# Where the first load stands in SyncE's opening instructions, in a ReLU-and-sum kernel on one core

## The chip, the cores and the metric

The kernel runs on one core of one Trainium2 chip. The metric is the time on the device in microseconds (us), the median of several executions. The span of a profile is another thing: it goes from the start of the first to the end of the last instruction that the profile ties to the kernel's source. In every profiled run of this case the time is 1.3 to 1.4 us longer than the span. "Faster" and "slower" mean a difference of over 2%, with 95% intervals.

## The reference

```python
def setup_inputs():
    batch, seq, dim = 32, 512, 1024
    return {"x": np.random.randn(batch, seq, dim).astype(np.float32)}

def reference(x):
    relu_x = np.maximum(x, 0)
    return np.sum(relu_x, axis=-1).astype(np.float32)
```

The input is 16,384 rows of 1,024 float32 values, 67.11 MB. The output is one number for each row.

## The kernel before

SyncE issues all loads and stores. The first seven loads bring 16 rows for each of 128 partitions (8.39 MB) into one of three buffers; the last 16 rows of each partition come as 8, 4, 2 and 1 rows, and the very last row in four pieces. ScalarE clamps the rows, VectorE sums them, or either does both for single rows. The first three loads wait for nothing; the fourth waits for the first buffer to come free (in the trace VectorE's first sum ends at 53.16 us and the fourth load is issued at 53.18).

The program opens with a block of its own, ahead of the kernel's body. In the trace of the kernel before it shows as four memsets on GpSimd, from 0.23 us on, and a barrier: each of the five engines has a drain, the last of them SyncE's, from 0.431 to 0.563 us, and after it come semaphore records: two of GpSimd at 0.590 and 0.668, then one of each other engine, SyncE's wait at 0.710 first, all ended by 0.772. In the program's text some register setup on SyncE stands there as well. The kernel edits that block after its body is written, and puts the first load into it, ahead of SyncE's part in the barrier:

```python
EARLY = 1
# ...
def issue_ahead_of_the_barrier(tc, n_loads):
    SP = mybir.EngineType.SP                      # SyncE
    blocks = tc.nc.main_func.blocks
    opening = blocks[0].instructions
    body = next(b for b in blocks if b.name == tc.start_bb_name).instructions
    loads = [i for i in body if i.engine == SP][:n_loads]
    for i in loads:
        assert isinstance(i, mybir.InstDMACopy)
        body.remove(i)
    at = next(
        n
        for n, i in enumerate(opening)
        if i.engine == SP and isinstance(i, mybir.InstDrain)
    )
    opening[at:at] = loads
```

This is safe because the load needs nothing of another engine: it reads the input and writes a buffer that nobody has touched. At that moment SyncE's part of the opening block is this list (the order is that of the program's text):

```text
MOVE             (a register)
BASE_LOAD        (the base address)
MOVE             (a register)
MOVE             (a register)
MOVE             (a register)
MOVE             (a register)
DRAIN
EVENT_SEMAPHORE  (the wait at the barrier)
branch to the kernel's body
```

## Time and profile before

| | before |
|---|---|
| time, median of 3 runs | 161.31 us (161.17 to 161.50) |
| span of the profiled run | 160.01 us |

The prediction reads the parts of the span and shows the lines for the shares and for the stages. A packet is one of the pieces in which a transfer moves; the profiled run has 2,592. The view of one source line adds what the opening of the program left in the profile. Its columns are line, engine, operation and count, then the shortest, median and longest record in ns, and the first and last start in us; a q behind an engine's name stands for its sequencer (the last column is for shapes, which these don't have):

```profile
L255 DVEq DRAIN  x1: 10/10/10, 0.1 to 0.1; - x1
L255 ACTq DRAIN  x1: 8/8/8, 0.1 to 0.1; - x1
...
L255 SPq DRAIN  x1: 132/132/132, 0.4 to 0.4; - x1
L255 SPq EVENT_SEMAPHORE  x1: 17/17/17, 0.7 to 0.7; - x1
```

The generated opening has records under one line, L255, and instructions as short as 8 ns are among them. SyncE has two of them, the drain and the wait, and no register move.

### The profile page before, as it was taken

To read this page: it belongs to the slowest core of one execution; us is meant where nothing else is said; L and a number is where in the kernel's file an instruction comes from. 1 tells how busy PE (TensorE), PEld (TensorE's weight loads), DVE (VectorE), ACT (ScalarE), POOL (GpSimd) and SP (SyncE) were. 2 spreads that over 40 slices of the span, in tenths; PEclk is the share of its full clock that TensorE was granted. 3 is DMA by queue.
4 is the path that set the end of the run, shared out by engine and by line. 5 is a ranking of instruction groups with operands and counts; after the bars stand their busy time and mean duration, and the time that the engine had idled before them with its cause. 6 is when DMAs were issued, how large, how long until landed. Compare 5 with 4: busy or idle time off the path is not lost.

```text
span 160.0 us, 135 instructions
## 1 busy us (share of the span) xinstructions
DVE 117.7 (74%) x43; ACT 104.2 (65%) x50; POOL 0.2 (0%) x4
## 2 busy tenths in 40 slices
DVE  0000000009999499994999999999999999999995
ACT  3000049990699808996099951999339992499993
POOL 0000000000000000000000000000000000000000
DMA  7996996996996997999979969969969969898993
GB/s 262 524 508 279 524 492 295 524 491 295 524 491 295 524 442 344 524 393 393 524 344 442 524 262 524 524 262 524 524 262 524 491 295 524 377 410 385 428 405 109
DMA packets 2592, 67.18 MB, mean 420 GB/s; under 512 B 672, under 2 KB 1184, under 8 KB 1312
## 3 DMA queue, kind: packets, MB, share of 16 engines
q1 hardware_dynamic: 2592, 67.18, 98.0%
HBM read 67.11 MB, written 0.07 MB: 420 GB/s over the span
## 4 chain that ended last, share of the span: by engine, by line
DMA 43%; DVE 33%; ACT 17%; another core or an unknown queue 3%; SPq 1%; issue 0%
DVE res L124 32%; DMA io<-in_x_dram 25%; DMA piece<-in_x_dram 18%; ACT io L116 17%; SPq L98 1%; DVE piece L141 1%; DVE piece L209 0%
## 5 line engine op out<-in xcount | busy, mean ns | idle before, releaser
L124 DVE TENSOR_REDUCE res<-io 128x8 f32<-128x8192 f32 (+2 forms) x9 | 101.1, 11291 | 40.2 <-ACT io L116 40.2
L116 ACT ACTIVATE io<-io 128x8192 f32<-128x8192 f32 (+2 forms) x9 | 81.7, 9111 | 47.2 <-DMA io<-in_x_dram 47.2
L131 ACT ACTIVATE io<-io 128x1024 f32<-128x1024 f32 x20 | 20.9, 1045 | 5.4 <-DMA io<-in_x_dram 5.3
L141 DVE TENSOR_SCALAR_CACHE_REDUCE io<-io 128x1024 f32<-128x1024 f32 x13 | 15.1, 1225 | 0.2
L131 ACT ACTIVATION_READ_ACCUMULATOR io<-io 128x1 f32 x20 | 3.7, 187 | 0.0
L116 ACT ACT_TABLE_LOAD x1 | 1.3, 1283 | 0.8 <-PEq L255 0.8
L141 DVE TENSOR_SCALAR_CACHE_REDUCE piece<-piece 128x244 f32<-128x244 f32 (+2 forms) x3 | 1.2, 415 | 0.5 <-DMA piece<-in_x_dram 0.5
L141 DVE DVE_READ_ACCUMULATOR io<-io 128x1 f32 x13 | 1.2, 93 | 0.0
L209 DVE TENSOR_SCALAR_CACHE_REDUCE piece<-piece 128x271 f32<-128x271 f32 x1 | 0.4, 435 | 0.0
L141 DVE DVE_READ_ACCUMULATOR piece<-piece 128x1 f32 x3 | 0.2, 83 | 0.0
L255 POOL MEMSET const-bfloat16-1.0<- 128x1 bf16 x1 | 0.1, 103 | 0.0
L255 POOL MEMSET const-uint8-127<- 128x1 uint8 x1 | 0.1, 103 | 0.0
L255 POOL MEMSET const-float32-1.0<- 128x1 f32 x1 | 0.1, 100 | 0.0
L255 POOL MEMSET const-float32-0.0<- 128x1 f32 x1 | 0.1, 99 | 0.2 <-issue 0.2
L209 DVE DVE_READ_ACCUMULATOR piece<-piece 128x1 f32 x1 | 0.1, 82 | 0.0
## 6 DMA issues: line engine op xcount, KB each, us to landing
io<-in_x_dram SPq DMA_DIRECT2D x1, 4096.0 KB, 21.6
io<-in_x_dram SPq DMA_DIRECT2D x1, 2048.0 KB, 26.1
io<-in_x_dram SPq DMA_DIRECT2D x1, 1024.0 KB, 28.1
io<-in_x_dram SPq DMA_DIRECT2D x1, 512.0 KB, 28.9
piece<-in_x_dram SPq DMA_DIRECT2D x1, 134.0 KB, 28.4
piece<-in_x_dram SPq DMA_DIRECT2D x1, 130.0 KB, 28.6
piece<-in_x_dram SPq DMA_DIRECT2D x1, 126.0 KB, 28.7
piece<-in_x_dram SPq DMA_DIRECT2D x1, 122.0 KB, 28.8
```

What stands on the lines that cost most here:

```text
L98: dma = nc.sync.dma_start(out=dst, in_=src)
L116: i = nc.scalar.activation(out=ap, in_=ap, func=RELU)
L124: nc.vector.tensor_reduce(out=res[:, m : m + n], in_=ap, axis=mybir.AxisListType.X, op=ADD).wait_op(sems.act, n_act, "sem-ge").then_inc(se ...
L131: i = nc.scalar.activation(out=ap, in_=ap, func=RELU, accum_out=res[:, m : m + 1])
L141: i = nc.vector.tensor_scalar(out=ap, in0=ap, scalar1=0.0, scalar2=None, op0=MAX, op1=ADD, accum_out=accum_out,)
L209: nc.vector.tensor_scalar(out=last[:, :], in0=last[:, :], scalar1=0.0, scalar2=None, op0=MAX, op1=ADD, accum_out=res[:, NT - 1 : NT],).wai ...
L255: nc = _bacc.Bacc("TRN2", target_bir_lowering=False, num_devices=1)
```

## The change

The intent: the load uses none of the six instructions at the head of SyncE's list, so it need not wait for them. It is to be SyncE's very first instruction.

```diff
-    at = next(
-        n
-        for n, i in enumerate(opening)
-        if i.engine == SP and isinstance(i, mybir.InstDrain)
-    )
+    at = next(n for n, i in enumerate(opening) if i.engine == SP)
     opening[at:at] = loads
```

## The prediction

> **What bounds the kernel now.** I read the page's busy shares first, then the table by stage, then the timeline of the start and of the end, and last the list of what each engine waited for. The page says that neither compute engine is full and that the transfers are:
>
> ```profile
> span 160.0 us, 135 instructions
> DVE 117.7 (74%) x43; ACT 104.2 (65%) x50; POOL 0.2 (0%) x4
> ...
> q1 hardware_dynamic: 2592, 67.18, 98.0%
> HBM read 67.11 MB, written 0.07 MB: 420 GB/s over the span
> ```
>
> VectorE works for 74% of the span, ScalarE for 65%, and the packets of the one DMA queue fill 98% of the time of the 16 engines. The table by stage shows where the missing 2% are (columns: stretch, its length, busy time of VectorE, ScalarE and GpSimd, granted clock, DMA share, GB/s):
>
> ```profile
> 0.00:1.00 1.00, 0.00 (x0) 0.21 (x1) 0.20 (x4) 1.00 0.00 0
> 1.00:4.00 3.00, 0.00 (x0) 1.07 (x1) 0.00 (x0) 1.00 1.03 350
> 4.00:156.00 152.00, 115.62 (x34) 101.42 (x46) 0.00 (x0) 1.00 1.00 432
> 156.00:160.00 4.00, 2.07 (x10) 1.53 (x4) 0.00 (x0) 1.00 0.40 110
> ```
>
> For the 152 us in the middle the DMA share is 1.00 at 432 GB/s: nothing but the transfer of the 67.11 MB input counts there. The first microsecond moves no byte, and the last four have a share of 0.40. I looked at the packets one by one: the first starts 1.02 us after the span's start, the last of the input ends at 157.70, and between these two there is not one moment without a packet in flight. So the kernel is a lead-in of 1.02, a stream of 156.68 (67.11 MB / 156.68 us = 428 GB/s), and a tail of 160.01 - 157.70 = 2.31 (the last sums, the last store, its landing). A change at the start of the program can reach the lead-in alone. The lead-in, in the timeline of SyncE's queue and of the others:
>
> ```profile
> 0.00 1.60 SPq L98 DMA_DIRECT2D io<-in_x_dram  x3
> 0.23 0.10 POOL L255 MEMSET const-float32-0.0<- 128x1 f32 x1 [0.23 <-issue]
> ```
>
> The span's zero is the issue of the first load itself: no SyncE instruction that the profile ties to the kernel's source stands before it. In the trace this first issue lasts 0.383 us; SyncE's drain for the opening barrier follows at 0.431, the barrier lets SyncE go at 0.71, and the second load is issued at 0.792. That is 20 us before the first load is in (ScalarE starts on it at 22.05), so the barrier is hidden behind the first transfer.
>
> [...] The trace[...] has 25 records on SyncE, 18 transfers, 6 semaphore instructions and 1 drain, and SyncE's compiled stream is 29 entries, these 25 and 4 markers of starts and branches. Not one register move is in either. [...] here the first packet starts at 1.02, which is 0.64 after its issue ends at 0.383[...]. [...] A semaphore instruction on SyncE lasts 17 ns in this trace.
>
> **The change part by part.** *Intended:* the first load goes from a place just ahead of SyncE's drain to the place of SyncE's first instruction. In the list of the opening block, as the kernel's code sees it when it makes the move, six SyncE instructions lie between the two: five register moves and one loading of the base address. [...]
>
> *What is left of it:* nothing in the load uses these six, and nothing else in the program does. The built program of the kernel before has none of them any more: the opening block ends up with 23 instructions, and SyncE's are the load, the drain, the wait of the barrier and the branch. They are removed after the kernel's code has made its move, in both versions. I compared the built programs engine by engine: the same instructions in the same order on all five engines, and only line numbers differ (the new file is four lines shorter). In the list of the new kernel the load stands ahead of GpSimd's four memsets and of the others' barrier instructions, where it stood behind them, but these are other engines' streams. I also compared what the compiler writes for each engine: the five instruction files are equal byte for byte.
>
> *Sum:* removed 0 instructions, added 0, moved 0 on any engine. Lead-in 1.02, stream 156.68 and tail 2.31 stay, so the span stays at 160.0 and the time at 161.31. I choose 161.3.
>
> **The rivals.** *First rival: the six instructions are executed, and the profile hides them.* For it: the profile shows only records tied to a source line, the span begins at the load, and the timed 161.37 of the profiled run is 1.36 us longer than its span of 160.01, so there is room ahead of the first record. Then the load would come 0.1 us (six at 17 ns)[...] earlier, the whole stream would move with it because it has no gap, and the time would fall to 161.0 to 161.2. Against it: the opening semaphore instructions and drains, which come from the same generated opening and carry the line L255, are in the trace, and moves of that origin would be too; and the compiled streams don't contain them.
>
> *Second rival: the load meets something else at the very start.* If it really were issued earlier, it would run before the other engines have arrived at the barrier, and SyncE's drain, which comes after the issue, would come earlier too[...]. The barrier is hidden behind 20 us of transfer, so this can neither gain nor cost. For a slowdown by over 2% (3.2 us) the stream itself would have to lose its 428 GB/s, and no byte, buffer, queue or wait of it is touched.
>
> *Third rival: the placing of code or data changes.* All buffers are allocated in the same order, and the streams are equal, so I give this almost nothing; a difference would be one between chips or runs.
>
> **Range and chances.** With nothing changed, the spread is that of repeated runs: 161.17 to 161.50, that is -0.09% and +0.12% about the median. A median of other runs, perhaps on another chip, should lie within about 0.35% of this one: 160.75 to 161.9. The low side also holds what the first rival could give. A change of 2% is 3.2 us, more than three times the whole lead-in of 1.02, so even a load that cost nothing at its start could not reach it: 0.98 for within 2%, and 0.01 for either side.
>
> **What would show it right or wrong.** The page of the changed kernel should have 135 instructions again, a span of 160.0 within 0.3, its zero at the first load's issue, the drain on SyncE at about 0.43 and the second load at about 0.79. First packet at 1.02 and no gap to about 157.7 would confirm the sum. If the first rival is true, the span stays (it starts at the load) but the time falls by 0.1 to 0.3 with it unchanged, so that the difference of 1.36 between the two gets smaller. The prediction would be wrong if the program that runs were built otherwise than the one I compared, with the moves kept, or if the stream's rate differed between the two.

The terms of its estimate for the six instructions came to 0.29 us, 0.2% of the time; one of them was measured in no trace. What is left with that estimate in it, the 161.0 of the first rival and the upper end of "0.1 to 0.3" here and in the first two expectations below (so also the 161.6 of the first), is the author's estimate; the lower end is six times the 17 ns that a semaphore instruction's record on SyncE lasts in the trace. The experiments measured 0.377 us. The forecast's own sum, lead-in 1.02, stream 156.68 and tail 2.31, comes to 160.01 us of span and 161.3 of time.

## The result, and the profile after

| | before | changed |
|---|---|---|
| time, median of 6 runs each | 161.30 us (161.13 to 161.50) | 161.26 us (161.18 to 161.58) |
| ratio, 95% interval | | 1.0001 (0.9988 to 1.0013) |
| span of the profiled run | 160.01 us | 159.83 us |
| first packet | 1.02 us | 1.02 us |
| second load issued | 0.792 us | 0.800 us |
| first buffer full, ScalarE starts | 22.05 us | 21.84 us |

A ratio is the mean time of one kernel's runs over that of the other's runs of the same rounds, so it is not quite the ratio of the medians. The time is the same.

The page of the changed kernel has the same number of instructions and the same busy times:

```profile
span 159.8 us, 135 instructions
...
DVE 117.7 (74%) x43; ACT 104.2 (65%) x50; POOL 0.2 (0%) x4
```

Its table by stage agrees as well (stretch, length, busy time of VectorE, ScalarE and GpSimd, granted clock, DMA share, GB/s):

```profile
0.00:1.00 1.00, 0.00 (x0) 0.21 (x1) 0.20 (x4) 1.00 0.00 0
1.00:4.00 3.00, 0.00 (x0) 1.08 (x1) 0.00 (x0) 1.00 1.04 350
4.00:156.00 152.00, 115.80 (x34) 101.59 (x46) 0.00 (x0) 1.00 1.00 432
156.00:160.00 4.00, 1.89 (x10) 1.35 (x4) 0.00 (x0) 1.00 0.40 109
```

And so does the timeline of its start:

```profile
0.00 1.61 SPq L98 DMA_DIRECT2D io<-in_x_dram  x3
0.23 0.10 POOL L251 MEMSET const-float32-0.0<- 128x1 f32 x1 [0.23 <-issue]
```

The zero is the first load's issue, as before, and GpSimd's first memset starts 0.23 us after it, as before. Had the load really come earlier against the rest of the program, this distance would have grown; in the experiments below the load does move against that memset, to 0.14 us behind its start with the six ahead of the load and to 2.12 with forty instructions there. The opening's line is now L251, since the file is four lines shorter; SyncE still has one drain and one wait there and no move:

```profile
L251 SPq DRAIN  x1: 141/141/141, 0.4 to 0.4; - x1
L251 SPq EVENT_SEMAPHORE  x1: 17/17/17, 0.7 to 0.7; - x1
```

The two profiled spans differ by 0.18 us. All of it is there when the first transfer is in, 21.84 against 22.05, long after both first packets at 1.02. Equal programs differ by that much from run to run: the times of the six runs of the changed kernel go from 161.18 to 161.58.

### The profile page after: what moved, and what is told of

Read it like the earlier page. It is cut to its first block, busy times and chain, and to the rows that moved or that the text cites. A ratio compares the mean times of both kernels' runs of the same rounds, so it can differ in the third digit from the quotient of the medians.

```text
span 159.8 us, 135 instructions
## 1 busy us (share of the span) xinstructions
DVE 117.7 (74%) x43; ACT 104.2 (65%) x50; POOL 0.2 (0%) x4
## 3 DMA queue, kind: packets, MB, share of 16 engines
HBM read 67.11 MB, written 0.07 MB: 420 GB/s over the span
## 4 chain that ended last, share of the span: by engine, by line
DMA 43%; DVE 33%; ACT 17%; another core or an unknown queue 3%; SPq 1%; issue 0%
DVE res L124 32%; DMA io<-in_x_dram 25%; DMA piece<-in_x_dram 18%; ACT io L116 17%; SPq L98 1%; DVE piece L141 1%; DVE piece L209 0%
## 5 line engine op out<-in xcount | busy, mean ns | idle before, releaser
L251 POOL MEMSET const-bfloat16-1.0<- 128x1 bf16 x1 | 0.1, 101 | 0.0
L251 POOL MEMSET const-uint8-127<- 128x1 uint8 x1 | 0.1, 101 | 0.0
L251 POOL MEMSET const-float32-0.0<- 128x1 f32 x1 | 0.1, 98 | 0.2 <-issue 0.2
L251 POOL MEMSET const-float32-1.0<- 128x1 f32 x1 | 0.1, 98 | 0.0
```

Of the source, the lines that this page charges most:

```text
L251: nc = _bacc.Bacc("TRN2", target_bir_lowering=False, num_devices=1)
```

## The experiments

The prediction says that the change moved nothing, as the six instructions are in neither program. Since the two compiled streams are equal byte for byte, the comparison is one of a program with itself, if what was compared is what ran. A result of "the same" fits that, but it alone would fit two other stories too: that the six are executed without records and cost too little to be seen, or that the place of the first load does not matter at all. The experiments put real instructions where the six had been thought to be.

### Keeping the six alive, with the load behind them

A use of the registers that the six instructions set is added to the kernel before, behind the third load, where SyncE has nothing to do for 51.6 us anyway. The use itself leaves no instruction, but the six now stay in the program. SyncE's compiled stream grows from 29 to 35 entries; the other engines' streams stay equal byte for byte to those of before.

```diff
+        if j == NBUF - 1:
+            keep_preamble_alive(nc)
...
+def keep_preamble_alive(nc):
+    sp = nc.sync
+    regs = [sp.zero_reg, *sp.tpb_base_reg]
+    for pair in sp.bc_regs:
+        regs += list(pair)
+    sp.keepalive_nop(ins=[sp.lower_val_access(r) for r in regs])
```

> The kernel before, with the six opening instructions of SyncE (five register moves, one loading of the base address) kept alive by a use behind the third load, so that they are executed ahead of the first load. Theory (they were not in either program; executed they cost something): six new records on SyncE ahead of the load, span and time longer by 0.1 to 0.3 us, 161.4 to 161.6, against 161.3. Rival (they are executed in the kernel before as well and only lack a record): the time stays at 161.3 and the first records stay as they were.

Measured: 161.50 us (161.44 to 161.71, 5 runs), before 161.25, ratio 1.0018 (1.0006 to 1.0031). The page counts six more instructions, and the view of the opening's line (L265 here) names them, as MOVE and BASE_LOAD:

```profile
span 160.4 us, 141 instructions
```

```profile
L265 SPq MOVE  x5: 29/29/40, 0.0 to 0.3; - x5
...
L265 SPq BASE_LOAD  x1: 12/12/12, 0.1 to 0.1; - x1
...
L265 SPq DRAIN  x1: 128/128/128, 0.8 to 0.8; - x1
```

The timeline puts the load behind them:

```profile
0.38 1.72 SPq L98 DMA_DIRECT2D io<-in_x_dram  x3
```

In the trace the six start at 0, 0.097, 0.144, 0.198, 0.257 and 0.307, and the load at 0.377; the first packet is at 1.386. So these instructions do leave records when they are executed, and they do cost time. The rival that the kernel before executes them unseen falls: it has neither the records nor the time.

### Keeping the six alive, with the load ahead of them

This is the changed kernel with the same addition, so the only difference to the experiment above is the diff under study.

> The changed kernel with the same six kept alive: the load is ahead of them. Theory: this is what the change was meant to do; the six run between the load and the drain, the barrier is later by their 0.1 to 0.3 us, hidden behind the first 20 us of transfer; time 161.3, so 0.1 to 0.3 less than with the load last. Rival (the place of the load does not matter even when the six are there): no difference between the two.

Measured: 161.36 us (161.25 to 161.56, 5 runs), ratio to before 1.0008 (0.9995 to 1.0020). The load is at zero again, and the six stand behind it:

```profile
0.00 1.95 SPq L98 DMA_DIRECT2D io<-in_x_dram  x3
```

```profile
L261 SPq MOVE  x5: 29/29/40, 0.4 to 0.8; - x5
...
L261 SPq BASE_LOAD  x1: 42/42/42, 0.5 to 0.5; - x1
L261 SPq DRAIN  x1: 7/7/7, 0.8 to 0.8; - x1
```

The first packet is at 1.004. But 161.36 against 161.50 is 0.14 us, and both intervals overlap: too little to tell the two places apart. So both were run again.

> Second set of runs of the kernel before with the six opening instructions kept alive, since the first set gave 161.50, 0.25 over before, where its trace has the load 0.38 us after the first of the six. Theory (one for one, blurred by some 0.2 us of spread in the stream): over both sets 0.25 to 0.45 above before, 161.5 to 161.7. Rival (a part of the six is hidden): again 161.5 or less.

> Second set of runs of the changed kernel with the six kept alive. Theory: as before, 161.2 to 161.35, so 0.25 to 0.45 less than with the load last. Rival (no difference between the two places): the same as the kernel with the load last.

Measured, on another chip: 161.62 us (161.39 to 161.69) with the load last and 161.26 (161.18 to 161.29) with the load first, before 161.27; ratios 1.0018 (1.0005 to 1.0032) and 0.9998 (0.9985 to 1.0010). Over both sets, ten runs each, the means are 161.58 and 161.32, and 161.28 for the 18 runs of before. The standard deviation is 0.12 in either ten, so the difference of 0.26 us has a standard error of 0.12 x sqrt(2/10) = 0.05. The place of the load matters when the six are there, and putting it first takes back what they cost, within 0.1 us. The traces of the second set agree: the load is at 0.377 and at 0 again. With the load last the times are longer than before by 161.58 - 161.28 = 0.30, where the trace has 0.377; the standard error is 0.04, so these runs don't decide whether all of the 0.377 counts. The kernel with the load first is not faster than the kernel before; it has no reason to be, as that one has the load first already.

### A dose large enough to read: forty instructions ahead of the load

Forty increments of an unused semaphore stand ahead of the first load.

```diff
+    for _ in range(40):
+        nc.sync.sem_inc(sems.pad, 1)
...
-    loads = [i for i in body if i.engine == SP][:n_loads]
+    loads = [i for i in body if i.engine == SP][: n_loads + 40]
...
```

Left out here are the semaphore itself, its clearing at the end, and an assertion that each moved instruction is a load.

> Forty increments of an unused semaphore on SyncE ahead of the first load: a dose large enough to be read. At the 17 ns of one such record they take at least 0.7 us, at twice that 1.4. Theory (SyncE time ahead of the load counts one for one): the time is longer by just what the trace shows between their first start and the load, 162.0 to 162.7. Rival (the clock starts at the first load, so what lies ahead of it is free): 161.3.

Measured: 163.62 us (163.47 to 163.70, 4 runs), ratio 1.0146 (1.0130 to 1.0161). The trace has the load behind the increments (six of the forty stand under the opening's line, L257, and not under L35):

```profile
L35 SPq EVENT_SEMAPHORE  x34: 17/17/17, 0.4 to 2.3; - x34
```

```profile
2.36 1.59 SPq L101 DMA_DIRECT2D io<-in_x_dram  x3
```

The forty take 2.364 us in the trace, and the time is longer by 163.60 - 161.27 = 2.33 (means of the same rounds). SyncE's time ahead of the first load counts one for one, within the spread of the runs, and it counts in the metric, not just in the span. The expectation had 0.7 to 1.4 us for the forty, which was too little: the record of such an instruction is 17 ns long, but the next one starts 59 ns after its start, on average (2.364 us / 40).

### The same forty behind the load

```diff
+    loads = loads[40:] + loads[:40]
```

> The same forty increments on SyncE between the first load and its drain: the barrier and the second load are later by 0.7 to 1.4 us, the first load is not. Theory (all behind the first load is hidden by its 20 us of transfer): 161.3, no stream gap. Rival (the barrier or the second issue is on the path): longer by as much as the barrier is later, 162.0 to 162.7.

Measured: 161.31 us (161.21 to 161.38, 5 runs), ratio 1.0001 (0.9987 to 1.0014). The forty stand between the first load, at zero, and ScalarE's first work, which waits for the barrier:

```profile
L35 SPq EVENT_SEMAPHORE  x40: 17/17/17, 0.4 to 2.7; - x40
```

```profile
0.00 3.83 SPq L101 DMA_DIRECT2D io<-in_x_dram  x3
...
3.02 1.28 ACT L119 ACT_TABLE_LOAD   x1 [3.02 <-PEq L258]
```

ScalarE's first work comes at 3.02 us, where it came at 0.79 before: the barrier is 2.2 us later, and so is the second load (3.016). The time does not show it. This pair of kernels is the change of this document, with forty real instructions in the place of the six: load behind them 163.62, ahead of them 161.31.

### No load ahead of the barrier, and three

`EARLY` is set to 0 and to 3 in the kernel before.

```diff
-EARLY = 1
+EARLY = 0
```

> No load ahead of the barrier: the first load waits for it. Theory (lead-in counts one for one): the span begins with a barrier record and the load is issued 0.6 to 0.7 us after that, so the span is about 0.6 longer: 161.9. Rival (the lead-in is hidden): 161.3.

Measured: 161.92 us (161.80 to 162.04, 5 runs), ratio 1.0041 (1.0028 to 1.0054). The load is issued at 0.731:

```profile
0.73 1.33 SPq L98 DMA_DIRECT2D io<-in_x_dram  x3
```

The difference is 161.934 - 161.269 = 0.665 us (means of the same rounds), near to the 0.731. So the kernel before already has the gain that a move of the first load ahead of the barrier brings: it is worth 0.4%.

> Three loads ahead of the barrier in place of one. Theory (only the first load's issue counts): 161.3, second and third load issued at about 0.4 and 0.8 us and not earlier in effect. Rival (the second load's issue matters, too): up to 0.1 us less.

Measured: 161.40 us (161.03 to 161.72, 6 runs), ratio 1.0012 (1.0000 to 1.0025). The second and third load are issued at 0.433 and 0.900 in the trace, where they were at 0.792 and 1.175, and the barrier lets go at 1.66 in place of 0.71. It gains nothing; the runs spread more than those of the other kernels, for a cause that no run here tells.

### The changed kernel once more

> The changed kernel once more, for the noise: ratio 1.000 within 0.1%, 161.2 to 161.4. If the program that runs were another one than before's, a shift of the same sign as any other job's would show.

Measured: 161.34 us (161.32 to 161.46, 4 runs), ratio 1.0006 (0.9992 to 1.0019). In the first comparison the changed kernel's median was below that of before, here it is above. That is what noise looks like, with ten runs of the changed kernel between 161.18 and 161.58.

No experiment points to a version that beats both kernels: of the places tried, the best for the first load is the one that both have.

## Why the prediction was right

**What bounds the kernel** was right. Forty instructions ahead of the load, 2.36 us long, made the time 2.33 us longer, and the same forty behind it did not change it. In the changed kernel, too, the packets of the input follow each other without a gap, from 1.02 to 157.57 us.

**The change part by part** was right in what decides: nothing removed, nothing added, nothing moved. This was no luck: it was read from the two compiled programs. The profile after shows it with 135 instructions, the same distances at the start, and no move on SyncE. The experiment that keeps the six alive shows that "no record" really meant "not executed". What took them away is seen in the programs: in the text that the kernel edits they are there, in the built program they are not, and one use of their registers is enough to bring all six back. The runs don't tell more of the step that drops them.

**The estimate of the six, 0.29 us,** is a term that was mis-sized, though the 161.3 did not rest on it; the first rival's 161.0 to 161.2 did. It was made of 17 ns for each move and of a term for the loading of the base address that no trace showed. Measured, the six take 0.377 us: a move is followed by the next instruction after 50 to 97 ns, not 17, and the loading of the base address by the next after 47 ns, which was less than its term. In the timed runs the six cost 0.30 us. The 17 ns are the length of a semaphore instruction's record, and the prediction took it for the distance to the next instruction.

**The first rival** (executed, but hidden) had 1.36 us between time and span in its favour, and said that this would shrink if it were true. In the changed kernel's profiled run it was 161.18 - 159.83 = 1.35. With the six alive that difference was 161.71 - 160.37 = 1.34 us: the six went into the span, not into the remainder. What the remainder holds stays open.

**The second rival** (the barrier or the second load comes into play) was rightly set aside, and the forty behind the load are a harder test of it than the change could be. **The third** (code or data placed otherwise) found no support: the repeat gave 1.0006 with an interval that holds 1.

**The range,** 160.75 to 161.9, held every single run of the changed kernel and not only the median; the ten runs spread from 161.18 to 161.58, so it was wide on both sides. The argument against 2% was right too: even 2.36 us of instructions ahead of the load make 1.5%.

## What to carry to other kernels

Before you price the removal or the move of an instruction, look for it in the trace and in the built program, and compare the two builds engine by engine: a list that your code edits is not yet the program, and of a move in it only the order within one engine's stream came through here. In a kernel that is one long transfer, look at the time that the issuing engine spends ahead of the first load: here 2.36 us of it cost 2.33, while the same 2.36 us behind the load cost nothing that the runs can tell, as the first transfer lasted to 22 us. How much more would have been free behind it was not tried. When a change gives "the same", put a large dose of the supposed cost in the disputed place: forty instructions gave a difference of 2.33 us, where the six took two sets of runs to show one of 0.3.

## What the traces add on SyncE and the load

- On SyncE, semaphore increments followed each other every 59 ns on average (forty in 2.36 us), and a register move was followed by the next instruction after 50 to 97 ns, with the load last. Their records, of 17 ns and of 29 to 40 ns, are shorter than that.
- With the load last, the instruction after the loading of the base address started 47 ns later.
- The kernel's list has six instructions of register setup on SyncE, its trace none; with a use of their registers added, the trace has 141 instructions in place of 135.
- In the kernel before, the input streams at 428 GB/s (67.11 MB in 156.68 us). No run here had a second core that transfers at the same time.
- The first packet of the kernel before is 1.02 us after the start of the first load's issue and 0.64 after its end.
- Right behind a load's issue, SyncE's drain lasts 132 ns (before), 141 (changed) and 128 (the six ahead of the load); with the six between the load and the drain, 7 ns. So the six, which take 0.41 us there, made the barrier later by only 0.975 - 0.710 = 0.27 us.
